# A gate folded into a product's weights by GpSimd, and a sum taken straight from PSUM

## The chip, the cores and the metric

The kernel runs on one core of one Trainium2 chip. The time is device time in microseconds (us) for one execution of the whole program. The five engines of the core (TensorE, VectorE, ScalarE, GpSimd, SyncE) each work through their own queue in order, and wait for one another by semaphores. In the profile PE is TensorE, PEld its weight loads, DVE VectorE, ACT ScalarE, POOL GpSimd, SP SyncE, which issues most transfers.

## The reference

One encoder block on 512 tokens of width 2048, in float32. Two token mixers (dilated window attention and chunked gated linear attention) read one normalised input; their gated outputs `a_out` and `g_out` are joined to 512 x 2048 and go through one output projection. What matters here is the end:

```python
y = jnp.concatenate([a_out, g_out], axis=-1) @ w_out[layer]
x = x + gate[:, None] * y
return rms_norm(x) * final_gain
```

`gate` is a vector of 2048, one factor per output column, the same for every token. So the factor of a column may be applied to that column of the product, or to that column of `w_out` ahead of the product.

## The kernel before

**Precision.** Each float32 operand is split into a high part, rounded to the format that TensorE takes at full rate, and a low part, the rest. ScalarE makes the high part (L493, in split_hi), VectorE the low one (L477, in split_lo). A product is then three matmuls: high times high, low times high, high times low (`three`, L231 to L233).

**The output projection.** The 2048 output columns are four column blocks j of 512, taken in two pairs, OUT_PAIRS = ((0, 1), (3, 2)). Each pair is computed by seven half-size products in place of eight (a Strassen scheme), in the order P1, P7, P6, P4, P5, P3, P2. Each product has four steps g; a step needs one block of weights of 128 x 1024 (two slices of 128 contracted rows by 512 columns). The blocks of the projection are numbered O0 to O55; O28 to O55 belong to the second pair, and O48 to O51 are P3's, O52 to O55 are P2's, the last product of all. P2's result goes to column block 3 only (`l` = 3), for row blocks 0 and 1 (128 tokens each). Row blocks 2 and 3 are finished during P3.

**How a block of weights arrives.** SyncE issues its load (L390) as soon as one of eight raw buffers is free; the last four blocks' loads wait for the low-half split of the block that used the buffer before. Then come the high half on ScalarE, into one of three buffers that TensorE must have left, and the low half on VectorE. The very first block of P2, O52, has buffers of its own, called `wlast`.

**The end.** While P3 runs, row blocks 2 and 3 get their last column block added (add_rest, L1611 to L1613) and are finished: `finish` makes the reciprocal root on ScalarE (L1585, L1586, into `rn`), scales on VectorE (L1595), ScalarE (L1596, L1598) and GpSimd (L1597), and stores. P2 then runs for row block 0 on 512 columns (accumulator `g3[0]`), and for row block 1 in two halves of 256 columns, each with an accumulator of its own, so that the first half can be added while TensorE works on the second. Row block 0 is added by add_rest and finished by finish_first. Row block 1 is added by add_half (L1644 multiplies the gate into the PSUM result, L1645 adds that to x), called once by first_half and once by finish_last, which also takes the sum of squares (L1658), makes the reciprocal root and scales and stores what is left. `gate_b` holds the gate on all 128 partitions; it is in place long before.

**Order.** TensorE's order is that of the program. On the other engines the compiler's scheduler chooses the order among the instructions that are ready, except in the parts under `tc.manual_schedule(engines=PLANNED)`, such as first_half and finish_last, which keep the order in which they are written. `last["hi"]` and `last["lo"]` chain the splits.

Of the kernel before, what the change touches and what calls it, by code (L numbers as in the profile page):

```python
# [13 lines left out]
AF = mybir.ActivationFunctionType  # L14
ALU = mybir.AluOpType
# [3 lines left out]
P = 128  # L19
# [112 lines left out]
OUT_PAIRS = ((0, 1), (3, 2))  # L132
# [60 lines left out]
def block_kernel(ctx: ExitStack, tc: tile.TileContext, a: dict):  # L193
    nc = tc.nc
# [20 lines left out]
    def PJ(name):  # L215
        return pp.tile([P, 512], F32, tag="pj", bufs=5, name=name)

    def PA(name):
        return pp.tile([P, 512], F32, tag="pa", bufs=3, name=name)

    mm = nc.tensor.matmul
    tt = nc.vector.tensor_tensor
    stt = nc.vector.scalar_tensor_tensor
    act = nc.scalar.activation
# [134 lines left out]
    groups = [(u, g) for u in ("qk2", "qk4", "qk6", "gk") for g in range(KT // 2)]  # L359
# [4 lines left out]
    raws, wts, low, last = {}, {}, set(), {}  # L364

    def fetch(i):
        if i < len(groups) and i not in raws:
            u, g = groups[i]
            if u == "O":
                raws[i] = out_fetch(g)  # L370
            elif u == "V":
                raws[i] = val_fetch(g)
            else:
                raws[i] = RAW(f"raw_{u}{g}", [2, 512])
                nc.sync.dma_start(raws[i], a["w_" + u][g])
# [86 lines left out]
    def whole(i):  # L462
        if i in second:
            t, e = raws[i], second.pop(i)
            tt(t, t, e, op=ALU.add)
# [14 lines left out]
    def split_hi(i):  # L480
        if i < len(groups) and i not in wts:
            fetch(i)
            u, g = groups[i]
            raw = raws[i].rearrange("p k c -> p (k c)")
            whole(i)
            dst = None
            if (u, g) == ("O", len(groups) - gi["O", 0] - 4):
                t = b8.tile([P, 2, 1024], F32R, tag="b8", name="wlast")
                dst = t[:, 0, :], t[:, 1, :]
            wts[i] = dst or (wp.tile([P, 1024], F32R, tag="whi", name=f"{u}{g}h"),  # L490
                             wp.tile([P, 1024], F32R, tag="wlo", name=f"{u}{g}l"))
            with tc.issue_after(last["hi"]) if u in ("V", "O") else nullcontext():
                last["hi"] = act(wts[i][0], raw, AF.Copy).ins  # L493
# [205 lines left out]
    for i in range(n):  # L699
        if i > 15:  # L700
            mm_task(i)
        st, k, j = chain[i]
# [14 lines left out]
    for i in range(n, 2 * n):  # L717
        mm_task(i)
        st, k, j = chain[i]
# [3 lines left out]
    for w in range(4):  # L723
        for kt in range(4):
            j, g = w // 2 * 4 + kt, w % 2
# [293 lines left out]
    def some_sums(name):  # L1019
        r = [sum_work.pop(0) for _ in range(SUMS_IN.get(name, len(sum_work)))]  # L1020
        n = len(r)
        loads = [(max(q - 1.1, 0.05) / n, x[0]) for q, x in enumerate(r)]
        return sorted(loads + [((q + 0.7) / n, x[1]) for q, x in enumerate(r)], key=lambda x: x[0])
# [278 lines left out]
    for n, p in (("qk2", 0), ("qk4", 2), ("qk6", 4)):  # L1302
        ps = unit(n, False, attention((p, p + 1)) + ([(0.05, shift_row)] if p == 2 else []))
# [9 lines left out]
    ps = unit("gk", False, attention((6, 7)) + [(0.88, lr_load)])  # L1313
# [138 lines left out]
    for j in range(2):  # L1452
        ps = unit(f"ag{j}", False, gla_head(1 + j) + some_sums(f"ag{j}"))
        gate_evict(ps, cat[j], f"a{j}", vbias[:, 4 * j:4 * j + 4])
    ps = unit("gg0", False, gla_head(3) + some_sums("gg0"))
# [44 lines left out]
    ps = unit("gg1", False, side + some_sums("gg1"))  # L1500
    gate_evict(ps, cat[3], "g1")
    mid.close()
    op = ctx.enter_context(tc.tile_pool(name="op", bufs=1, reuse_waits="tile"))
    for e in "hl":
        t = hp.tile([P, KT, 512], F32R, tag="h", name="c_" + e)
# [4 lines left out]
    gate_b = op.tile([P, 2048], F32, tag="gate", name="gate_b")  # L1510
# [11 lines left out]
    def E_(name):  # L1522
        return op.tile([P, 512], F32, tag="e", bufs=3, name=name)

    xo, x_pair, fgain = {}, {}, {}
    ssq = cst.tile([P, 4, 4], F32, tag="ssq", name="ssq")
# [23 lines left out]
    def keep(name, ps):  # L1550
        r = []
        for n, p_ in enumerate(ps):
            t = op.tile([P, 512], F32, tag="keep", bufs=7, name=f"{name}{n}")
            act(t, p_, AF.Copy)
            r.append(t)
        return r
# [12 lines left out]
    def summed(ps, kept, op_):  # L1569
        return lambda t: tt(t, ps, kept, op=op_)  # L1570

    def negated(ps, kept):
        return lambda t: stt(t, ps, -1.0, kept, op0=ALU.mult, op1=ALU.subtract)

    def first_squares(i, js):

        s = ssq[:, i, js[0]:js[0] + 1]
        for j in js[1:]:
            tt(s, s, ssq[:, i, j:j + 1], op=ALU.add)
        nc.vector.tensor_scalar(s, s, 1.0 / D, EPS, op0=ALU.mult, op1=ALU.add)  # L1580
        return s
# [26 lines left out]
    def add_rest(i, j, ps, op_):  # L1608

        x_, t = xo[i, j], E_(f"y{i}{j}")  # L1610
        tt(t, ps, gate_b[:, 512 * j:512 * j + 512], op=ALU.mult)  # L1611
        tt(x_, x_, t, op=op_)
        act(t, x_, AF.Square, accum_out=ssq[:, i, j:j + 1])  # L1613
# [21 lines left out]
    half_e = {}  # L1635

    def add_half(i, j, ps, z):

        c = slice(256 * z, 256 * z + 256)
        x_ = xo[i, j][:, c]  # L1640
        if not z:
            half_e[i] = E_(f"y{i}{j}")
        t = half_e[i][:, c]
        tt(t, ps, gate_b[:, 512 * j + 256 * z:512 * j + 256 * z + 256], op=ALU.mult)  # L1644
        tt(x_, x_, t, op=ALU.add)  # L1645
        return x_, t

    def first_half(i, j, ps, s):
        x_, t = add_half(i, j, ps, 0)
        act(t, x_, AF.Square, accum_out=ssq[:, i, j:j + 1])  # L1650
        tt(xo[i, 2], xo[i, 2], fgain[2], op=ALU.mult)
        stt(s, ssq[:, i, j:j + 1], 1.0 / D, s, op0=ALU.mult, op1=ALU.add)
# [77 lines left out]
    def more(pair, prod, g, fn, *args):  # L1730
        later(pair, prod, g, lambda: fn(*args))
# [6 lines left out]
    for pair, (l, r) in enumerate(OUT_PAIRS):  # L1738
        end = pair == 1
        g1 = [PA(f"g1{pair}{n}") for n in range(2)]  # L1740
        product(pair, "P1", g1, True, True)
        p1 = keep(f"p1{pair}", g1)
        gx = [PJ(f"gx{pair}{n}") for n in range(2)]
        product(pair, "P7", gx, True, True)
        p7 = keep(f"p7{pair}", gx)
        if end:
            for n in range(2):
                more(pair, "P6", n, x_with, n, l, p1[n], ALU.add)
                more(pair, "P6", 2 + n, x_with, 2 + n, r, p7[n], ALU.subtract)
        product(pair, "P6", g1, False, True)  # L1750
        u2 = keep(f"u2{pair}", g1)
        product(pair, "P4", gx, False, True)
        for n in range(2):
            more(pair, "P5", 1 + 2 * n, add_up, 2 + n, l, summed(gx[n], u2[n], ALU.add), True)
        product(pair, "P5", g1, False, True)
        v = keep(f"v{pair}", g1)
        for n in range(2):
            if not end:
                more(pair, "P3", 2 * n, add_up, 2 + n, r, negated(g1[n], p7[n]), True)
            else:  # L1760
                more(pair, "P3", 2 * n, add_rest, 2 + n, r, g1[n], ALU.subtract)
                more(pair, "P3", 2 * n + 1,
                     lambda n=n, l=l, r=r: finish(2 + n, r, first_squares(2 + n, [0, 1, l])))
        g2 = [PJ(f"g2{pair}{n}") for n in range(2)]
        product(pair, "P3", g2, True, True)
        if end:
            for i in range(gi["O", 0] + 2 * 4 * len(OUT_ORDER) - 3, len(groups)):
                split(i)
        for n in range(2):
            more(pair, "P2", n, add_up, n, r, summed(g2[n], v[n], ALU.subtract), not end)  # L1770
            if end:
                more(pair, "P2", n, sum_squares, n, [0, 1, r])
        g3 = [PJ(f"g3{pair}0"), PA(f"g3{pair}1")] + [PJ(f"g3{pair}2")] * end
        if not end:
            product(pair, "P2", g3, True, True)
            for n in range(2):
                more(pair + 1, "P1", 2 * n, add_up, n, l, summed(g3[n], p1[n], ALU.add), True)
            continue
        product(pair, "P2", g3, True, True, (0,))
        add_rest(0, l, g3[0], ALU.add)  # L1780
        finish_first(0, sq0[0])
        ah, al = ops["A12"]
        for z in range(2):
            c0, t = 256 * z, slice(P, 2 * P)
            for k in range(8):
                wh, wl = wts[gi["O", (pair * len(OUT_ORDER) + OUT_ORDER.index("P2")) * 4 + k // 2]]
                c = slice(512 * (k % 2) + c0, 512 * (k % 2) + c0 + 256)
                three(g3[1 + z][:, :256], ah[:, k, t], al[:, k, t], wh[:, c], wl[:, c], k == 0, k == 7)
        with tc.manual_schedule(engines=PLANNED):
            first_half(1, l, g3[1][:, :256], sq0[1])  # L1790
            finish_last(1, l, g3[2][:, :256], sq0[1])
# [71 lines left out]
```

## Time and profile before

| What | Value |
|---|---|
| median of 3 runs | 900.62 us (900.61 to 900.75) |
| the profiled execution | 900.47 us |
| its span in the profile | 898.7 us |
| TensorE busy | 889.1 us, 99% of the span |
| VectorE busy | 732.3 us, 81% |
| ScalarE busy | 500.9 us, 56% |
| GpSimd busy | 123.0 us, 14% |
| granted TensorE clock | 0.997 of full speed |

The span runs from the first to the last instruction that the profile shows; 1.8 us of the execution lie outside it. A share is the engine's busy time over the whole span, so it tells little of the last 40 us, where the edit lies. Busy time on TensorE is pipelined; a matmul's end is modelled. A wait is put down to the event that came last before it.

### The profile page before, as it was taken

The numbers are of one execution on the slowest core, as the hardware profiler recorded it, in microseconds if no ns is written. First come the engines' busy times: TensorE is split into PE (matmuls) and PEld (weight loads), VectorE is DVE, ScalarE is ACT, GpSimd is POOL, SyncE is SP. The second block draws the span as 40 slices with busy tenths as digits, with TensorE's granted clock in tenths as the row PEclk, the third lists the DMA queues.
The fourth block names the chain that finished last, engine by engine and source line by source line (L and its number), as shares of the span: only waits on it lengthen the run. The fifth ranks groups of instructions, "written<-read, shape, count | busy, mean of one in ns | idle before, by whom it ended". The sixth has DMA issues, their size and how long they took to land.

```text
span 898.7 us, 12367 instructions
## 1 busy us (share of the span) xinstructions
PE 889.1 (99%) x4190; PEld 741.5 (83%) x4190; DVE 732.3 (81%) x1221; ACT 500.9 (56%) x859; POOL 123.0 (14%) x219
## 2 busy tenths in 40 slices
PE   9999999999999999999999999999999999999996
PEld 7888788888888888888878888888888888888885
DVE  7998799878989989889668668595775749997797
ACT  5553533466755756756767554363644447655564
POOL 0000000024423333233100102111020100000001
PEclk9999999999999999999999999999999999999998
DMA  9998589398698899898878879678787898877853
GB/s 358 399 413 358 197 345 366 132 306 229 198 266 266 231 285 260 236 316 225 272 239 267 313 204 307 206 250 258 234 275 219 253 322 295 278 295 252 304 210 148
DMA packets 65547, 242.33 MB, mean 270 GB/s; under 512 B 9190, under 2 KB 11526, under 8 KB 55883
## 3 DMA queue, kind: packets, MB, share of 16 engines
q1 hardware_dynamic: 58724, 199.23, 61.5%
q0 software_dynamic: 6464, 42.01, 19.9%
q8 instruction: 33, 0.54, 0.2%
q10 hardware_dynamic: 296, 0.30, 0.1%
q14 instruction: 30, 0.25, 0.1%
HBM read 224.64 MB, written 51.47 MB: 307 GB/s over the span
## 4 chain that ended last, share of the span: by engine, by line
PE 98%; ACT 0%; DVE 0%; ACTq 0%; issue 0%
PE ps_qk L231 5%; PE ps_qk L233 5%; PE ps_qk L232 5%; PE g L231 4%; PE g L232 4%; PE g L233 4%; PE stb L233 3%; PE ps_gg L231 3%; PE ps_ag L231 3%; PE ps_ag L232 3%; PE ps_gg L232 3%; PE stb L232 3%; PE ps_ag L233 3%; PE ps_gg L233 3%; PE stb L231 3%; PE o L928 3%
## 5 line engine op out<-in xcount | busy, mean ns | idle before, releaser
L863 POOL TENSOR_SCALAR p<-p,st 128x32 f32<-128x32 f32 (+2 forms) x108 | 57.8, 544 | 160.2 <-DVE st L853 88.6
L327 DVE CUSTOM_DVE_ANT_0 cb<-cb,sb,c_bcond 128x2048 f32<-128x2048 f32 (+1 forms) x32 | 73.7, 2303 | 1.5 <-DMA cb<-in_wm 0.9
L850 ACT ACTIVATE p<-p,st 128x416 f32<-128x416 f32 x64 | 41.1, 642 | 56.0 <-DVE st L846 48.4
L428 POOL DMA_DIRECT2D T<-in_w_o x32 | 23.2, 724 | 155.4 <-ACT V2h L493 12.0
L886 ACT ACTIVATE pth<-t 128x384 fp32r<-128x384 f32 x64 | 30.9, 483 | 13.1 <-PE t L880 8.0
L887 DVE TENSOR_TENSOR ptl<-t,pth 128x384 fp32r<-128x384 f32 x64 | 35.2, 550 | 3.3 <-ACT pth L886 2.4
L880 PE MATMUL t<-c_ident,p 128*128 128x128 f32 x192 | 31.3, 272 | 0.0
L880 PEld LDWEIGHTS t<-c_ident,p 128*128 128x128 f32 x192 | 24.3, 139 | 7.8
L846 DVE CUSTOM_DVE_ANT_0 p<-s,g,st 128x256 f32<-128x256 f32 x64 | 27.7, 433 | 2.0
L846 DVE CUSTOM_DVE_ANT_0 p<-s,g 128x160 f32<-128x160 f32 x64 | 23.5, 368 | 4.6 <-PE s L839 4.2
L1597 POOL TENSOR_SCALAR x<-x,rn 128x512 f32<-128x512 f32 x2 | 2.9, 1444 | 146.0 <-ACT rn L1586 142.1
L428 POOL DMA_DIRECT2D T3V<-in_w_gv x8 | 5.5, 692 | 125.1 <-ACT qk21h L493 118.7
L838 PE MATMUL s<-ks,qh 128*128 128x416 f32 x64 | 22.5, 352 | 0.0
L327 DVE CUSTOM_DVE_ANT_0 rawg<-rawg,crow,gate 128x1024 f32<-128x1024 f32 x16 | 20.4, 1278 | 2.6 <-DMA rawg<-in_wg 2.5
L839 PE MATMUL s<-ks,ql 128*128 128x416 f32 x64 | 22.4, 350 | 0.0
L1104 ACT ACTIVATE sq<-st,sc 128x256 f32<-128x256 f32 x24 | 12.1, 505 | 17.3 <-DVE st L1099 8.9
L327 DVE CUSTOM_DVE_ANT_0 rawg<-rawg,crow,c_bcond 128x1024 f32<-128x1024 f32 x16 | 20.3, 1279 | 1.0 <-issue 1.0
L909 ACT ACTIVATE pth<-g 32x128 fp32r<-32x128 f32 x64 | 19.7, 308 | 1.6
L428 POOL DMA_DIRECT2D T<-T x16 | 9.1, 572 | 79.4 <-ACT V8h L493 13.0
L567 ACT ACTIVATE h_hi<-xt,shift 128x512 fp32r<-128x512 f32 x16 | 11.5, 722 | 10.3 <-DVE shift L327 9.5
L1372 DVE TENSOR_TENSOR vS<-rawS,vS 128x1024 fp32r<-128x1024 f32 x8 | 9.7, 1224 | 8.7 <-ACT vS L1371 8.5
L533 ACT ACTIVATE h_hi<-xt,scale 128x512 fp32r<-128x512 f32 (+1 forms) x18 | 12.5, 703 | 6.9 <-DVE scale L327 6.9
(1672 smaller groups left out, 3172.6 us busy)
## 6 DMA issues: line engine op xcount, KB each, us to landing
cb<-in_wm SPq DMA_DIRECT2D x31, 1024.0 KB, 11.4
T<-in_w_o POOLq DMA_DIRECT2D x32, 512.0 KB, 6.1
rawg<-in_wg SPq DMA_DIRECT2D x32, 512.0 KB, 5.3
raw_O<-in_w_o SPq DMA_DIRECT2D x32, 512.0 KB, 5.3
raw_qk<-in_w_qk SPq DMA_DIRECT2D x24, 512.0 KB, 4.9
raw_O<-T SPq DMA_DIRECT2D x24, 512.0 KB, 5.8
rawb<-in_w_sb SPq DMA_DIRECT2D x16, 512.0 KB, 7.9
rawv<-in_wv SPq DMA_DIRECT2D x16, 512.0 KB, 6.1
```

The lines of the kernel that those rows point to most:

```text
L231: mm(ps, lh, rh, start=first, stop=False, skip_group_check=more)
L232: mm(ps, ll, rh, start=False, stop=False, skip_group_check=more)
L233: mm(ps, lh, rl, start=False, stop=last, skip_group_check=more)
L327: return nc.vector.tensor_tensor_reduce(out=w, in0=w, in1=with_, op0=ALU.mult, op1=ALU.add, scale=1.0, scalar=init, accum_out=dst)
L428: move = nc.gpsimd.dma_start(dst, src, max_dma_last_dim=8192, **how).ins
L846: top = nc.vector.tensor_tensor_reduce(out=t[:, lo:hi], in0=ps[:, lo:hi], in1=gt[h][:, at:at + 2 * (hi - lo) - 1:2], op0=ALU.add, op1=ALU.min,
L850: act(t, t, AF.Exp, bias=st[:, 0:1], scale=-1.0, accum_out=st[:, 1:2])
L863: last["pool"] = nc.gpsimd.tensor_scalar(to, of, st[:, 2:3], 1.0, op0=ALU.mult, op1=ALU.mult).ins
L880: nc.tensor.transpose(pk[:, n_ * P:n_ * P + P], t[:, first_ + kt * P:first_ + kt * P + P], ident)
L886: act(hi, src, AF.Copy)
L887: tt(lo, src, hi.bitcast(F32), op=ALU.subtract)
L928: mm(po[:, P * a0:P * a1], vv[h // 4][:, c, h % 4, :], pt[:, at:at + (a1 - a0 - 1) * step + 1:step, :], start=n_ == z == 0, stop=False, sk ...
```

## The change

In split_hi, for the four blocks O52 to O55 (P2 of the second pair), GpSimd multiplies columns 256 to 511 of both slices of the raw block by the gate of column block 3, in place, ahead of the split into high and low halves. It is one instruction a block, on 128 x (2 x 256) elements; the gate operand is one row of 256 on each partition, read twice.

The second half of P2's result thus holds the gate already. add_half with z = 1 adds PSUM to x directly and leaves out the product with the gate. Row block 0 must take its two halves in different ways too, so the new add_parts stands in the place of add_rest: for z = 0 product and sum, for z = 1 the sum alone, then the Square with its sum as before.

```diff
@@ split_hi
             whole(i)
+            if u == "O" and i >= len(groups) - 4:
+                l = OUT_PAIRS[1][0]
+                g_ = gate_b[:, 512 * l + 256:512 * l + 512]
+                part_ = raws[i][:, :, 256:512]
+                nc.gpsimd.tensor_tensor(part_, part_, g_.unsqueeze(1).broadcast_to([P, 2, 256]), op=ALU.mult)
@@ add_half
         t = half_e[i][:, c]
-        tt(t, ps, gate_b[:, 512 * j + 256 * z:512 * j + 256 * z + 256], op=ALU.mult)
+        if z:
+            tt(x_, x_, ps, op=ALU.add)
+            return x_, t
+        tt(t, ps, gate_b[:, 512 * j:512 * j + 256], op=ALU.mult)
         tt(x_, x_, t, op=ALU.add)
         return x_, t
+
+    def add_parts(i, j, ps):
+
+        x_ = xo[i, j]
+        for z in range(2):
+            add_half(i, j, ps[:, 256 * z:256 * z + 256], z)
+        act(half_e[i], x_, AF.Square, accum_out=ssq[:, i, j:j + 1])
@@ the last pair, after P2 for row block 0
         product(pair, "P2", g3, True, True, (0,))
-        add_rest(0, l, g3[0], ALU.add)
+        add_parts(0, l, g3[0])
         finish_first(0, sq0[0])
```

## The prediction

> **What bounds the kernel now.** I read the page's busy shares first, then the chain of waits in its last 15 us, then the timelines of the engines around them.
>
> ```profile
> PE 889.1 (99%) x4190; PEld 741.5 (83%) x4190; DVE 732.3 (81%) x1221; ACT 500.9 (56%) x859; POOL 123.0 (14%) x219
> ```
>
> The whole is bound by TensorE. No matmul is added or removed, so only two things can move the time: a stall of TensorE, and what runs after its last matmul. The chain of waits shows that second stretch (start, us, what):
>
> ```profile
> 891.02 0.13 PE g L233
> 891.15 0.02 issue
> 891.17 0.44 DVE y L1644
> ...
> 891.63 0.44 DVE x L1645
> 892.09 0.48 DVE y L1658
> ```
>
> From 891.15, the end of the last matmul, everything is serial: gate product (L1644), sum into x (L1645), sum of squares (L1658), rsqrt, scaling, store. One link that goes shortens the end by its pitch, as long as nothing else arrives later. So the question is who else is nearly late. VectorE's timeline (start, us, engine, line, operation, tiles, shapes; in brackets the idle time before and its releaser):
>
> ```profile
> 867.30 1.23 DVE L477 TENSOR_TENSOR O49l<-raw_O,O49h 128x1024 fp32r<-128x1024 f32 x1 [0.63 <-ACT O49h L493]
> 869.16 0.69 DVE L1612 TENSOR_TENSOR x<-x,y 128x512 f32<-128x512 f32 x1
> 870.02 1.23 DVE L477 TENSOR_TENSOR O50l<-raw_O,O50h 128x1024 fp32r<-128x1024 f32 x1 [0.17 <-ACT O50h L493]
> 871.76 0.74 DVE L1595 SCALAR_TENSOR_TENSOR x<-x,rn,fgain 128x512 f32<-128x512 f32 x1
> 872.42 1.10 DVE L1612 TENSOR_TENSOR x<-x,y 128x512 f32<-128x512 f32 x1
> 873.99 1.23 DVE L477 TENSOR_TENSOR O51l<-raw_O,O51h 128x1024 fp32r<-128x1024 f32 x1 [0.47 <-ACT O51h L493]
> 875.56 1.23 DVE L477 TENSOR_TENSOR wlast<-raw_O,wlast 128x1024 fp32r<-128x1024 f32 x1 [0.34 <-ACT wlast L493]
> 876.70 1.22 DVE L477 TENSOR_TENSOR O53l<-raw_O,O53h 128x1024 fp32r<-128x1024 f32 x1
> 877.83 1.18 DVE L1595 SCALAR_TENSOR_TENSOR x<-x,rn,fgain 128x512 f32<-128x512 f32 x1
> ...
> 881.27 1.21 DVE L477 TENSOR_TENSOR O55l<-raw_O,O55h 128x1024 fp32r<-128x1024 f32 x1
> ...
> 885.67 0.68 DVE L1611 TENSOR_TENSOR y<-g,gate_b 128x512 f32<-128x512 f32 x1
> 886.39 0.69 DVE L1612 TENSOR_TENSOR x<-x,y 128x512 f32<-128x512 f32 x1
> ...
> 888.43 0.49 DVE L1628 TENSOR_SCALAR x<-xg,rn 128x512 f32<-128x512 f32 x1 [0.57 <-ACT rn L1586]
> ...
> 890.33 0.16 DVE L1652 SCALAR_TENSOR_TENSOR ssq<-ssq 128x1 f32<-128x1 f32 x1
> 891.17 0.42 DVE L1644 TENSOR_TENSOR y<-g,gate_b 128x256 f32<-128x256 f32 x1 [0.68 <-PE g L233]
> ```
>
> VectorE has almost no room. From 867 on its waits are 0.63, 0.17, 0.47 and 0.34, then none up to 0.57 ahead of L1628, and 0.68 ahead of the closing L1644. The 0.57 gives nothing back: L1628 waits for a chain (Square, two activations) that starts from VectorE's own L1612, so it moves with it. **Slack to the end: 0.68 us**, and no more.
>
> **The change, part by part.** *Removed at the end.* For row block 1, second half, the gate product goes and x takes PSUM directly: one instruction of 128x256 with one operand in PSUM, as L1644 has. It saves the pitch 891.17 to 891.63: **0.46 us**, all of it on the chain.
>
> *Row block 0* (add_parts for add_rest) has three 128x256 operations in place of two of 128x512. Before: 885.67 to the end of L1612 at 887.08, 1.41. After: by L1644's 0.42 each, with start distances of about 0.42 to 0.46, 1.3 to 1.4. I cost it at nothing. The Square behind it is unchanged.
>
> *Added: four products on GpSimd*, each 128x512 elements with two SBUF operands (weight half, gate), ahead of the split of blocks O52 to O55. When can they run? SyncE's timeline, its waits and the landing times of line 390:
>
> ```profile
> 856.15 1.80 SPq L390 DMA_DIRECT2D raw_O<-in_w_o  x2
> 860.68 0.33 SPq L390 DMA_DIRECT2D raw_O<-in_w_o  x1
> 863.06 0.33 SPq L390 DMA_DIRECT2D raw_O<-in_w_o  x1
> SPq L390 <- DVE O47l L477: 2.0, 1, 2.0
> DMA to landing us min/median/max: 3.4/4.4/5.2
> ```
>
> These four loads land between 856.15 + 3.4 = 859.6 and 863.06 + 5.2 = 868.3 (the last waits for O47l to free its buffer, so it slips with VectorE). GpSimd is empty there:
>
> ```profile
> 871.74 1.25 POOL L1597 TENSOR_SCALAR x<-x,rn 128x512 f32<-128x512 f32 x1 [142.11 <-ACT rn L1586]
> 876.84 1.64 POOL L1597 TENSOR_SCALAR x<-x,rn 128x512 f32<-128x512 f32 x1 [3.85 <-DVE wlast L477]
> ```
>
> So the products should run from about 861 to 870. The new wait is that of the high halves on ScalarE (L493): the first of them, wlast, starts only at 874.48, so 4 us of cover hide the wait (ScalarE's timeline):
>
> ```profile
> 873.87 0.61 ACT L1613 ACTIVATE y<-x 128x512 f32<-128x512 f32 x1
> ...
> 874.48 1.05 ACT L493 ACTIVATE wlast<-raw_O 128x1024 fp32r<-128x1024 f32 x1
> 875.43 0.27 ACT L1585 ACTIVATE rn<-ssq 128x1 f32<-128x1 f32 x1
> 875.61 1.04 ACT L493 ACTIVATE O53h<-raw_O 128x1024 fp32r<-128x1024 f32 x1
> 876.56 0.18 ACT L1586 ACTIVATE rn<-rn 128x1 f32<-128x1 f32 x1
> ...
> 879.75 1.06 ACT L493 ACTIVATE O55h<-raw_O 128x1024 fp32r<-128x1024 f32 x1 [0.69 <-PE g L232]
> ```
>
> Queued behind it on ScalarE stand the rsqrt of block 3 (L1585, L1586) and O53h; they would wait only if a product came after 874.5.
>
> *What a product does to VectorE.* VectorE's rows above show it at the GpSimd rows. L1612 takes 1.10 beside the first, 0.69 without; L1595 takes 1.18 beside the second, 0.74 without. The ends fit one reading: GpSimd's instruction waits for the running VectorE instruction (O53l ends at 877.92), runs about 0.56 to 878.48, and only then L1595 proceeds, to 879.01. A 128x512 GpSimd instruction of one operand thus delays VectorE by 0.41 to 0.44. [...]
>
> *Price of a two-operand product.* No row has one. Low end: that of one operand, 0.43. High end: the longest record above, 1.64, taken as if GpSimd held VectorE for all of it but the 0.13 by which the hold of 0.56 exceeds the delay of 0.43: 1.5. Between them I go by the grouped rows:
>
> ```profile
> L863 POOL TENSOR_SCALAR p<-p,st 128x416 f32<-128x416 f32 x16 | 9.8, 613 | 77.8 <-DVE st L853 43.6 <-PE s L839 17.1 <-issue 13.7
> L1097 POOL TENSOR_SCALAR dc<-st,sc 128x256 f32<-128x256 f32 x16 | 7.7, 479 | 29.1 <-DVE st L1094 24.1 <-DVE st L1099 4.9
> ```
>
> (613 - 479) / (416 - 256) = 0.84 ns per element, so a second operand of 512 elements adds 0.43: estimate **0.86 us a product**, nearest to the low end's rows. [...]
>
> *The sum.* VectorE in the stretch of the products is nearly always busy with two-operand SBUF work:
>
> ```profile
> 860.00:864.00 4.00, 4.00 (x19) 3.30 (x19) 4.00 (x6) 2.19 (x4) 0.00 (x0) 1.00 0.64 234
> 864.00:868.00 4.00, 4.00 (x20) 3.30 (x19) 3.22 (x8) 2.48 (x5) 0.00 (x0) 1.00 0.36 133
> 868.00:872.00 4.00, 4.00 (x19) 3.34 (x18) 3.80 (x6) 3.32 (x8) 0.26 (x1) 1.00 0.00 0
> ```
>
> (After the window's length stand TensorE, its weight loads, then VectorE: 4.00, 3.22, 3.80 of 4 us.) Four products: 4 x 0.86 = 3.44. Idle time takes up 0.63 (O49l) and 0.17 (O50l). Of 0.47 and 0.34 I count only 0.30 together: wlast's high half stands on ScalarE behind the Square of block 3 (L1613 at 873.87), which starts 0.35 after the end of L1612 at 873.52, about 0.05 of it latency, so ScalarE can yield only 0.30. VectorE's delay from 875.6 on: 3.44 - 0.63 - 0.17 - 0.30 = 2.34. It reaches the end unreduced, less the slack: 2.34 - 0.68 = 1.66 later, less 0.46 saved: **+1.20 us**.
>
> Does TensorE stall more? Its first uses of the low halves:
>
> ```profile
> 877.52 0.39 PE L233 MATMUL g<-O51l,c_h 128*128 128x512 f32 x1
> 884.32 0.39 PE L233 MATMUL g<-O55l,A12h 128*128 128x512 f32 x1
> ```
>
> O51l ends at 875.22, 2.30 ahead, and would slip 3.44 - 0.63 - 0.17 - 0.47 = 2.17: just in time. O55l ends at 882.48, 1.84 ahead, and slips 2.34: 0.5 of stall. TensorE would end 0.5 later, VectorE's queue is 1.66 beyond the old end; VectorE decides.
>
> The profiled execution took 900.47, the median is 900.62, 0.15 above. So 900.47 + 1.20 = 901.67, in terms of the median **901.8 us**. A measurement of this kernel can tell about 0.2%, 1.8 us, from no change; this is 0.13%.
>
> **The rivals.** *The products stay hidden.* If one delays VectorE by no more than (1.10 + 0.68) / 4 = 0.445, the delay ends within the slack and the 0.46 remains: 900.2. For it: the one-operand price of 0.43 is just below; a product beside L1611, which has one operand in PSUM, may cost little. Against: two operands, and 4.00 of 4 us busy.
>
> *GpSimd's order puts the products of O53 to O55 behind block 3's L1597*, which waits for rn; slower than before. From the point at which O53's product stands behind it this decides. L1597 ends at 878.48 and L1595 at 879.01; then products of 0.99 (0.56 + 0.43), with a VectorE instruction of 0.68 or 1.2 between: 880.0, about 881.7, about 883.9. O55h (1.06) and O55l (1.21) follow: 886.2 in place of 882.48, VectorE 3.7 late. 3.7 - 0.68 - 0.46 = +2.6: 903.2. For it: in the program L1597 of block 3 is written ahead of these splits. Against: the order is not the written one throughout (O53h at 875.61 stands between L1585 at 875.43 and L1586 at 876.56, though written after both), and the data are there 8 us before.
>
> *A dearer product* (1.0 to 1.5 each) with the order I expect: 4 x 1.0 - 1.10 - 0.68 - 0.46 = +1.8 up to 4 x 1.5 - 2.24 = +3.8, 902.4 to 904.4.
>
> **How the numbers follow.** Forecast (0.6 to 1.0 a product, 900.8 to 902.4) 0.50; hidden, 900.2 to 900.8, 0.25; dearer product 0.13; GpSimd's order 0.10; anything else, 0.02. The range 900.1 to 903.4 takes in the first two, the second rival and most of the dearer product, and leaves out some 0.07. Slower by over 0.2% (above 902.4): 0.13 + 0.10 + 0.01 = 0.24. Faster by over 0.2% needs 1.8 us where 0.46 is removed: 0.01. Same: 0.75.
>
> **What would show it.** Right: four GpSimd records of 128x512 between 861 and 871, VectorE instructions beside them 0.8 to 0.9 longer, the waits ahead of O49l and O50l gone, the closing L1645 started by VectorE's own L1652 instead of TensorE, 2 us after the last matmul or less. Wrong: the closing sum still starts 0.02 after TensorE's last matmul (hidden), products behind 878 with ScalarE waiting for GpSimd (the order), or TensorE gaps of over 0.5 ahead of O51l to O55l.

## The result, and the profile after

The changed kernel takes **901.94 us** (median of 22 runs), the kernel before 900.67 (22 runs beside them): ratio 1.0015, 95% interval 1.0009 to 1.0021. That is 1.27 us more, 0.14%; the interval, 0.8 to 1.9 us, lies above zero. The forecast was 901.8.

The profiled execution took 902.03, its span is 900.2. The columns are those of the prediction. From split_hi on the line numbers of the changed code are 5 higher than before, from add_half on 8 to 15 higher. First a part of the chain of waits near the end of the changed kernel:

```profile
892.59 0.60 DVE x L1666
893.19 0.13 DVE ssq L1667
893.33 0.34 DVE x L1650
893.67 0.02 issue
893.69 0.48 DVE y L1673
```

Before, the chain came from TensorE to the closing product; now it comes from VectorE's own queue (L1666, L1667), and the closing sum (L1650) is a single link. TensorE's timeline in the changed kernel shows where its last matmul ends:

```profile
892.39 0.28 PE L233 MATMUL g<-O55l,A12h 128*128 128x256 f32 x1
```

892.67, 0.57 ahead of the closing sum at 893.24. Then GpSimd's timeline of the changed kernel:

```profile
861.12 3.09 POOL L490 TENSOR_TENSOR raw_O<-raw_O,gate_b 128x512 f32<-128x512 f32 x2 [131.39 <-DMA raw_O<-in_w_o]
865.09 1.36 POOL L490 TENSOR_TENSOR raw_O<-raw_O,gate_b 128x512 f32<-128x512 f32 x1 [0.88 <-DMA raw_O<-in_w_o]
868.58 1.61 POOL L490 TENSOR_TENSOR raw_O<-raw_O,gate_b 128x512 f32<-128x512 f32 x1 [2.13 <-DVE ssq L1585]
```

The four products run from 861 to 870. The first and the third start when their block has landed; the second follows the first. The fourth is put down to VectorE's L1585, which had ended 0.7 us before, so what released it is not shown. VectorE's timeline of the changed kernel shows what lay beside them, and what became of it:

```profile
861.27 1.79 DVE L1568 TENSOR_TENSOR y<-y,gate_b 128x512 f32<-128x512 f32 x1
862.98 2.31 DVE L477 TENSOR_TENSOR O47l<-raw_O,O47h 128x1024 fp32r<-128x1024 f32 x1
865.21 1.78 DVE L1572 TENSOR_TENSOR x<-x,fgain 128x512 f32<-128x512 f32 x1
866.91 0.68 DVE L1569 TENSOR_TENSOR x<-y,x 128x512 f32<-128x512 f32 x1
...
868.95 1.78 DVE L1572 TENSOR_TENSOR x<-x,fgain 128x512 f32<-128x512 f32 x1
...
870.95 1.23 DVE L477 TENSOR_TENSOR O49l<-raw_O,O49h 128x1024 fp32r<-128x1024 f32 x1
...
875.15 0.99 DVE L1600 SCALAR_TENSOR_TENSOR x<-x,rn,fgain 128x512 f32<-128x512 f32 x1
876.07 0.68 DVE L1617 TENSOR_TENSOR x<-x,y 128x512 f32<-128x512 f32 x1
877.17 1.23 DVE L477 TENSOR_TENSOR O51l<-raw_O,O51h 128x1024 fp32r<-128x1024 f32 x1 [0.43 <-ACT O51h L498]
...
888.84 0.42 DVE L1652 TENSOR_TENSOR y<-g,gate_b 128x256 f32<-128x256 f32 x1
...
891.28 0.49 DVE L1633 TENSOR_SCALAR x<-xg,rn 128x512 f32<-128x512 f32 x1 [0.57 <-ACT rn L1591]
...
893.17 0.16 DVE L1667 SCALAR_TENSOR_TENSOR ssq<-ssq 128x1 f32<-128x1 f32 x1
893.24 0.41 DVE L1650 TENSOR_TENSOR x<-x,g 128x256 f32<-128x256 f32 x1
```

Four instructions are 1.1 us longer (1.79 and twice 1.78 against some 0.69, 2.31 against 1.23). The wait of 0.63 ahead of O49l is gone: it starts at 870.95 in place of 867.30. Row block 0 starts at 888.84 in place of 885.67, and the closing sum stands directly behind L1667.

### The profile page after: what moved, and what is told of

It is laid out like the page before. It is cut to its first block, busy times and chain, and to the rows that moved or that the text cites. A ratio compares the mean times of both kernels' runs of the same rounds, so it can differ in the third digit from the quotient of the medians.

```text
span 900.2 us, 12380 instructions
## 1 busy us (share of the span) xinstructions
PE 890.6 (99%) x4190; PEld 741.8 (82%) x4190; DVE 735.6 (82%) x1221; ACT 500.7 (56%) x859; POOL 127.3 (14%) x223
## 4 chain that ended last, share of the span: by engine, by line
PE 95%; DVE 2%; ACT 1%; issue 0%; ACTq 0%; DVEq 0%
PE ps_qk L231 5%; PE ps_qk L233 5%; PE ps_qk L232 5%; PE ps_gg L231 3%; PE stb L233 3%; PE ps_ag L231 3%; PE ps_ag L233 3%; PE stb L231 3%; PE ps_gg L232 3%; PE ps_ag L232 3%; PE ps_gg L233 3%; PE stb L232 3%; PE g L231 3%; PE g L232 3%; PE g L233 3%; PE o L933 3%
## 5 line engine op out<-in xcount | busy, mean ns | idle before, releaser
L490 POOL TENSOR_TENSOR raw_O<-raw_O,gate_b 128x512 f32<-128x512 f32 x4 | 6.1, 1520 | 134.4 <-DMA raw_O<-in_w_o 132.3
```

## The experiments

The theory on trial: the end gains one VectorE link of 0.46, and GpSimd's products hold VectorE up by more than its idle time and slack take in. The rivals: the new wait for GpSimd ahead of the splits costs the time; or the direct sum and the small operations do.

**direct_only: the end alone.** The changed kernel without its products; the gate is left out of the last 256 columns of P2's result.

```diff
-            if u == "O" and i >= len(groups) - 4:
...
-                nc.gpsimd.tensor_tensor(part_, part_, g_.unsqueeze(1).broadcast_to([P, 2, 256]), op=ALU.mult)
```

> The changed kernel without the four GpSimd products; the gate is thus left out of the last 256 columns of P2's result. Theory (the gain is one VectorE link at the end, the loss is GpSimd's products holding VectorE up): 0.46 under before, about 900.2 against 900.67; the closing sum starts 0.02 after TensorE's last matmul, and VectorE's waits ahead of O49l, O50l, O51l and wlast are back at about 0.63, 0.17, 0.47 and 0.34. Rival (the direct sum or the three small operations of row block 0 cost what was lost): it stays at 901 to 902.

900.16 (11 runs) against 900.52 (24 runs), ratio 0.9995, 0.9986 to 1.0004: 0.36 under, near the 0.46 expected, though the interval takes in no change. The profile says more. VectorE's timeline of this run:

```profile
867.26 1.22 DVE L477 TENSOR_TENSOR O49l<-raw_O,O49h 128x1024 fp32r<-128x1024 f32 x1 [0.63 <-ACT O49h L493]
...
885.64 0.41 DVE L1647 TENSOR_TENSOR y<-g,gate_b 128x256 f32<-128x256 f32 x1
885.98 0.41 DVE L1645 TENSOR_TENSOR x<-x,g 128x256 f32<-128x256 f32 x1
886.30 0.42 DVE L1648 TENSOR_TENSOR x<-x,y 128x256 f32<-128x256 f32 x1
...
891.14 0.42 DVE L1645 TENSOR_TENSOR x<-x,g 128x256 f32<-128x256 f32 x1 [1.00 <-PE g L233]
891.60 0.48 DVE L1668 CUSTOM_DVE_ANT_0 y<-x,ssq 128x256 f32<-128x256 f32 x1
```

The closing sum waits for TensorE again, and the sum of squares follows 0.46 after its start, not 0.92. The three small operations start 0.34 and 0.32 apart and end at 886.72, where the two large ones ended at 887.08; hence the wait for TensorE is 1.00, not 0.68. Neither the direct sum nor row block 0 costs anything, so the second rival falls.

**lock_only: the products alone.** The kernel before, with the four products written to a tile that nothing reads.

```diff
+            if u == "O" and i >= len(groups) - 4:
...
+                beside = op.tile([P, 2, 256], F32, tag="beside", bufs=1, name="beside")
+                nc.gpsimd.tensor_tensor(beside, part_, g_.unsqueeze(1).broadcast_to([P, 2, 256]), op=ALU.mult)
```

> The kernel before, with the same four two-operand GpSimd products beside it, written to a tile that nothing reads, so no engine waits for them and the result is the reference's. Theory (GpSimd holds VectorE up): the VectorE instruction beside each product is 1.09 longer as in the changed kernel, VectorE is about 3.1 late at row block 0 (here without the 0.32 that the three small operations saved), less 0.77 of slack: 2.3 above before, about 903.0. Rival (the loss comes from the new wait for GpSimd ahead of the splits): no loss, 900.7.

903.0 (8 runs) against 900.52 (24 runs), ratio 1.0026, 1.0016 to 1.0036: 2.5 above the kernel before, with no engine waiting for a product. VectorE's timeline of this run:

```profile
861.37 1.79 DVE L1569 TENSOR_TENSOR y<-y,gate_b 128x512 f32<-128x512 f32 x1
863.08 2.31 DVE L477 TENSOR_TENSOR O47l<-raw_O,O47h 128x1024 fp32r<-128x1024 f32 x1
...
893.62 0.16 DVE L1658 SCALAR_TENSOR_TENSOR ssq<-ssq 128x1 f32<-128x1 f32 x1
893.69 0.42 DVE L1650 TENSOR_TENSOR y<-g,gate_b 128x256 f32<-128x256 f32 x1
...
894.61 0.48 DVE L1664 CUSTOM_DVE_ANT_0 y<-x,ssq 128x256 f32<-128x256 f32 x1
```

The lengths are those of the changed kernel, and again the closing instruction stands behind VectorE's own L1658. So the products cost this much without any wait for them.

**one_operand and write_only: the same waits, another GpSimd instruction.** The changed kernel with another instruction in the place of the product: in one_operand the first of the two added lines, in write_only the second.

```diff
-                nc.gpsimd.tensor_tensor(part_, part_, g_.unsqueeze(1).broadcast_to([P, 2, 256]), op=ALU.mult)
+                nc.gpsimd.tensor_scalar(part_, part_, 1.0, 1.0, op0=ALU.mult, op1=ALU.mult)
+                nc.gpsimd.memset(part_, 0.0)
```

> The changed kernel with a one-operand GpSimd instruction on the same data at the same place (times 1.0), so every wait of the change is there; the gate is left out of the last 256 columns of P2's result. Theory (the price is the time for which GpSimd holds VectorE up): 0.43 a product as beside L1597, 1.7 in all, swallowed by idle time (about 1.1) and the slack of 0.77: 900.2. Rival (the wait for GpSimd ahead of the splits, whatever GpSimd does): 901.9 as in the changed kernel.

> The changed kernel with a GpSimd memset to zero in place of each product: the same waits, but nothing is read; the second half of P2's result is thus zero. If only a GpSimd instruction that reads SBUF holds VectorE up: VectorE's instructions beside the memsets keep 0.69 and 1.23, time 900.2. If any GpSimd instruction does: they are 0.3 to 0.5 longer, and the time is 900.2 all the same, within the slack. If the wait alone costs: 901.9.

899.92 and 900.09 (11 runs each) against 900.56 (21 runs), both ratios 0.9994, 0.9985 to 1.0003. With every wait in place the cost of the products is gone, so the wait as such is not the cause. VectorE's timeline of one_operand, then of write_only, at the same instructions:

```profile
862.80 1.10 DVE L1572 TENSOR_TENSOR x<-x,fgain 128x512 f32<-128x512 f32 x1
863.82 1.09 DVE L1569 TENSOR_TENSOR x<-y,x 128x512 f32<-128x512 f32 x1
```

```profile
861.79 1.22 DVE L477 TENSOR_TENSOR O47l<-raw_O,O47h 128x1024 fp32r<-128x1024 f32 x1
862.93 0.68 DVE L1572 TENSOR_TENSOR x<-x,fgain 128x512 f32<-128x512 f32 x1
```

With one operand they take 1.10 and 1.09 against 0.68 and 0.69, 0.41 longer each. (The other two products of that run began beside 128x1 instructions; O48l and O49l behind them are only 0.19 and 0.28 longer, 1.42 and 1.51 against 1.23.) The four memsets lie between 860.8 and 867.4, and no VectorE instruction is longer. So in these runs it is a GpSimd instruction that reads SBUF that holds VectorE up, and the product of two operands, 1.09, costs more than twice what the instruction of one operand costs.

**two_of_four: half the dose.** The changed kernel with the products of O53 and O55 alone.

```diff
-            if u == "O" and i >= len(groups) - 4:
+            if u == "O" and i >= len(groups) - 4 and i % 2:
```

> The changed kernel with products on O53 and O55 alone; the gate is left out of the second half of O52 and O54. Theory (delays add up on VectorE, idle time and slack at the end swallow the first part): 2 x 1.09 = 2.2, less about 1.1 to 1.3 of idle time and 0.32 of row block 0, is below the slack of 0.77, so nothing of it arrives: 900.2, as with no product at all. Rival (each product costs the end the same share): half way between 900.2 and 901.94, about 901.1.

900.02 (11 runs) against 900.52 (24 runs), ratio 0.9994, 0.9985 to 1.0003. Half the products cost the end nothing that can be measured. VectorE's timeline of this run, all of it some 0.7 later than in direct_only from O46l on (860.12 against 859.40):

```profile
863.64 1.79 DVE L1572 TENSOR_TENSOR x<-x,fgain 128x512 f32<-128x512 f32 x1
...
868.28 2.10 DVE L477 TENSOR_TENSOR O49l<-raw_O,O49h 128x1024 fp32r<-128x1024 f32 x1
...
891.86 0.42 DVE L1650 TENSOR_TENSOR x<-x,g 128x256 f32<-128x256 f32 x1 [0.32 <-PE g L233]
```

The two products make VectorE's instructions 1.10 and 0.87 longer, and of the 1.00 of slack in direct_only 0.32 is left. The end pays no fixed share per product; it pays what passes idle time and slack.

**early: the products elsewhere, three times.** GpSimd multiplies the second halves in a tile of their own during earlier products, stores them to DRAM, and the late loads of O52 to O55 take columns 256 to 511 from there.

```diff
+        if (pair, what) == (1, "21"):
+            src = block(pair, what, g)
+            nc.sync.dma_start(t[:, :, :256], src[:, :, :256])
+            d = gated[g]
+            nc.sync.dma_start(t[:, :, 256:512], bass.AP(d.tensor, d.offset, [[512, P], [256, 2], [1, 256]]))
...
+    def gate_weights(g):
...
+        nc.gpsimd.tensor_tensor(t, t, g_.unsqueeze(1).broadcast_to([P, 2, 256]), op=ALU.mult)
...
+        nc.sync.dma_start(d, t.rearrange("p k c -> p (k c)"))
```

> Same result as the changed kernel, the products elsewhere: during P5 of the first pair GpSimd multiplies the second halves of the four blocks in a tile of their own and they are stored to DRAM; the late loads of O52 to O55 take columns 256 to 511 from there. 2 MB more are read and 1 MB more written. Theory (what counts is that VectorE is full where the products lie and has no more than 0.8 of slack to the end): VectorE loses about 1.1 a product there, which TensorE does not feel, and the end has the 0.46: 900.2. Rival (the products or the additional transfers delay the splits of P5 or P3): TensorE gaps near P5, 901 or more.

908.92 (4 runs) against 900.52 (24 runs), ratio 1.0087, 1.0073 to 1.0101: a miss, and for a reason of the experiment's own. (It reads 1 MB more, four loads of 256 KB, not the 2 MB expected.) GpSimd's timeline, SyncE's waits and TensorE's waits of this run:

```profile
770.60 10.56 POOL L1748 TENSOR_TENSOR gated<-gated,gate_b 128x512 f32<-128x512 f32 x1 [41.16 <-DMA gated<-in_w_o]
```

```profile
SPq L1751 <- POOL gated L1748: 27.1, 4, 11.0
```

```profile
PE g L233 <- DVE O17l L484: 5.0, 1, 5.0
PE g L233 <- DVE O26l L484: 1.2, 1, 1.2
```

Each store stood in SyncE's queue waiting for GpSimd, up to 11.0 us, and the loads of the weights behind it waited too; TensorE waited 5.0 and 1.2 and ended 8.8 later than before (its last matmul starts at 899.66 against 890.86). So load and store went to GpSimd's own queue:

> Same result as the changed kernel. The four products run from the end of the first pair's P2 to P7 of the second pair, in one tile of their own; load, product and store of each stand on GpSimd's own queue, so nothing of them stands in SyncE's queue (where, in the run before, each store waited for GpSimd and held the loads of the weights behind it). The late loads of O52 to O55 take columns 256 to 511 from the stored result. Theory: VectorE has 1 to 3 us of idle time in every 10 there and the splits are 3 us ahead of TensorE, so nothing stalls, and the end has its 0.46: 900.2, closing sum 0.02 after the last matmul. Rival (the early place costs by itself): TensorE gaps between 800 and 850, 901 or more.

900.76 (11 runs) against 900.69 (15 runs), ratio 1.0000, 0.9991 to 1.0009. The expected gain of 0.46 is not there. The scheduler had drawn the products even further ahead, to 754 to 803, and in the profiled execution, a long one of 902.70, TensorE still waited 0.8 for O26l. So each load was held back to the second pair's P1 or P7:

> As the run before (same result as the changed kernel, products through GpSimd's queue into DRAM), but each load waits for a high half of the second pair's P1 or P7 on ScalarE, so that the products lie at 810 to 850, where VectorE is busy 7 to 9 us in 10, and not at 755 to 803 where it is full. Theory: no TensorE gap from them, VectorE caught up before 860, the closing sum 0.02 after the last matmul with about 1.0 of wait before it: 900.2, 0.4 to 0.5 under the kernel before. Rival (the place does not matter, an additional load and store do): 900.7 or more.

900.54 (11 runs) against 900.59 (21 runs), ratio 1.0002, 0.9993 to 1.0011; the changed kernel in the same series took 902.07 (after_again, 11 runs), ratio 1.0018, 1.0009 to 1.0027:

> The changed kernel itself beside the run above on one chip. Theory: 901.9, 1.7 above the version with early products.

In the profile of after_again the products met other VectorE instructions, and these are together longer by as much as in the first profile: 2.28 against 1.23, 1.78 and 1.77 against 0.69, and an instruction of 128x1 that takes 0.15 elsewhere:

```profile
868.12 1.28 DVE L1584 TENSOR_TENSOR ssq<-ssq 128x1 f32<-128x1 f32 x1
```

So the delay hardly depends on the VectorE instruction of two SBUF operands that is held up: 1.13 at 128x1, 1.08 at 128x1024 (2.31 against 1.23). VectorE's timeline of early_paced:

```profile
891.52 0.42 DVE L1652 TENSOR_TENSOR x<-x,g 128x256 f32<-128x256 f32 x1 [1.01 <-PE g L233]
891.98 0.48 DVE L1675 CUSTOM_DVE_ANT_0 y<-x,ssq 128x256 f32<-128x256 f32 x1
```

The end is as the theory says, 1.01 of wait and one link, but TensorE arrives 0.35 later than before (891.52 against 891.17). It lost 0.6 at O42l: its first matmul of O41l starts 0.30 earlier than before (850.02 against 850.32), its second of O42l 0.31 later (854.03 against 853.72). The profile of early, too, has a wait of TensorE at O42l (0.3 in both), although its last product ran at 815, so what causes it is not shown. With the same result early_paced is 1.5 faster than the changed kernel, so where the products stand accounts for the loss. Against the kernel before, the 0.4 to 0.5 expected cannot be measured: 900.54 lies between the theory's 900.2 and the rival's 900.7. No version with the right result is measurably faster than the kernel before.

## Why the prediction was right, point by point

*What bounds the end.* Right: VectorE's queue, with less than 1 us of slack, decides; lock_only shows the loss by itself. In its profile the sum of squares starts 2.3 later than before (894.61 against 892.09, less 0.20 by which that run was late at O46l). It lacks the link saved, 0.47, and the 0.32 gained at row block 0; less these, 2.3 becomes 1.5, what the changed kernel's profile shows.

*The place of the products and the new wait.* Right: 861 to 870, ahead of every L1602, and ScalarE never waits for one. The rival of GpSimd's order did not occur.

*The mechanism.* Right: a GpSimd instruction that reads holds VectorE up (0.41 in one_operand, and in the rows of before L1612 at 1.10 against 0.69); one that only writes does not (write_only, 0.68 stays 0.68). A VectorE instruction with an operand in PSUM was not held up where the kernel before has one beside such a GpSimd instruction: L846 of 128x256 at 390.37 takes 0.41 within the time of L863 (390.16 to 391.02), and 0.42 at 401.60, where GpSimd runs nothing.

*The price of a product.* Mis-sized: 0.86 by the slope of one-operand rows, measured 1.79 - 0.69, 2.31 - 1.23 and twice 1.78 - 0.69: 4.36 for four, 1.09 each. The rows of one operand could not show it: from one operand to two the delay grows by 0.68 (0.41 to 1.09), where the slope gave 0.43. The price thus lies where the prediction had put its rival of a dearer product (1.0 to 1.5); that rival's time of 902.4 or more did not come, because more of the delay was taken up than either sum allowed for.

*The rest of the sum.* The changed run was 0.10 late already at O46l (the first of these lines is of the kernel before, the second of the changed one), so shifts are taken less 0.10:

```profile
859.43 1.22 DVE L477 TENSOR_TENSOR O46l<-raw_O,O46h 128x1024 fp32r<-128x1024 f32 x1
859.53 1.22 DVE L477 TENSOR_TENSOR O46l<-raw_O,O46h 128x1024 fp32r<-128x1024 f32 x1
```

| Term | Predicted, us | Measured, us | From |
|---|---|---|---|
| four products | 3.44 | 4.36 | lengths above |
| taken up by idle time | 1.10 | 1.29 | 4.36 less 888.84 - 885.67 - 0.10 |
| row block 0, gained | 0 | 0.32 | 885.67 to 888.43 before, 888.84 to 891.28 after |
| slack to the end | 0.68 | 0.77 | start of L1652 (L1667 after) to closing start: 0.84 before, 0.07 after |
| link saved | 0.46 | 0.47 | closing start to L1658 or L1673: 0.92 before, 0.45 after |
| sum | +1.20 | +1.51 | the sum of squares: 893.69 - 892.09 - 0.10 = 1.50 |

So 0.92 too little for the products stood against 0.61 too little for what softens them. The medians differ by 1.27, and the interval of 0.8 to 1.9 takes in both sums. That the forecast came within 0.1 us of the measured change is luck: two errors, each a large part of the change, nearly cancelled. (The prediction held 1.8 us to be the least that can be told from no change; 22 runs on each side told 1.27.) "I cost it at nothing" for row block 0 was the second wrong step. Its three instructions of 256 elements, none of which needs the result of the one just ahead of it, start 0.34 and 0.33 apart; of the two of 512 before, the second needs the first, and starts 0.72 behind it.

The idle time, too, was not taken up where the prediction had it. The waits ahead of O51l and wlast, counted at 0.30, gave 0.05 (0.47 and 0.34 became 0.43 and 0.33), because ScalarE's high halves slipped with VectorE (O51h starts at 876.10 in place of 872.91). Some 0.9 went ahead of O49l and O50l, where 0.80 was counted. Of the rest, 0.17 comes from GpSimd's first scaling instruction (L1597, now L1602): it holds L1600 up by 0.25 (0.99 against 0.74), where before it held L1612 up by 0.42 (1.10 against 0.68).

*TensorE.* Stalls were predicted at 0.5 in all. It ends at 892.67 against 891.14 before (the last record there starts at 890.86 and takes 0.28): 1.53 later, or 1.4 without the common 0.10. VectorE's delay was 3.1, where the prediction had 2.17 at O51l and 2.34 at O55l, and passes the 2.30 and 1.84 that these had in hand. The longest waits of its weight loads in the changed kernel:

```profile
PEld g L233 <- DVE O51l L477: 0.9, 1, 0.9
PEld g L233 <- DVE O55l L477: 0.5, 1, 0.5
PEld g L233 <- DVE O49l L477: 0.3, 1, 0.3
```

A TensorE gap of over 0.5 ahead of O51l was named as a sign of being wrong, and it came: O51l's first matmul starts at 878.46, 0.86 after the one ahead of it, where 0.23 is usual. VectorE is 0.57 later still, so this did not show in the time; TensorE is the next bound, close behind.

## What to carry to other kernels

In these runs work on an idle GpSimd was not free where it read SBUF while VectorE ran instructions of two SBUF operands: a product of 128x512 with two operands cost VectorE 1.09 us, an instruction with one operand 0.41, a memset nothing. Price such work as VectorE time. That price can be read from the length of VectorE instructions beside GpSimd records already in a trace, but only for an instruction of the same kind; the rows of one operand gave 0.86 for the product that took 1.09. What such a delay costs is what exceeds idle time and slack up to the end, so half of the work can cost nothing measurable (two_of_four) and the whole more than it gains. Whoever moves the work should look at the queue of its transfers: in early a store that waited on SyncE for up to 11.0 us held up the loads behind it.

## What the runs showed of the hardware that was not expected

In two runs a product that was ready had to wait while several VectorE instructions started ahead of it: eight in early, where its record takes 10.56 us from 770.60, and six in early_pool:

```profile
776.47 9.02 POOL L1751 TENSOR_TENSOR gated<-gated,gate_b 128x512 f32<-128x512 f32 x1 [3.96 <-DMA gated<-in_w_o]
```

VectorE's instructions of 128x1024 went on every 1.14 us, none longer, until one with an operand in PSUM came (784.25 in early_pool) or VectorE had nothing to do (780.01 in early). The other products of these two runs are 1.30 to 1.76 long; those of 767.02 and 801.05 in early_pool came in behind the VectorE instruction that was running, and the instruction after that one takes 2.31 against 1.22 and 1.78 against 0.69. A run made for it put nine such products into the same stretch of the kernel before, reading O8 to O16:

```diff
+            if u == "O" and 8 <= g < 17:
...
+                nc.gpsimd.tensor_tensor(beside, raws[i][:, :, 256:512], g_, op=ALU.mult)
```

> The kernel before with nine GpSimd products (two operands, 128x512) that read the raw blocks O8 to O16 as they land and write a tile that nothing reads, in the stretch in which VectorE has one 128x1024 instruction of two SBUF operands after another (755 to 782 in the kernel before). If GpSimd gets its turn at the end of the running VectorE instruction, as at 861 to 870: no product longer than 1.2 + 1.1 = 2.3, each VectorE instruction behind it 1.1 longer, VectorE up to 9 late and TensorE stalled behind it. If it can be passed over as long as VectorE's next such instruction stands ready: products of 5 us and more, few VectorE instructions longer, little time lost.

It took 906.59 (a single run, against 900.69 in 15 runs). GpSimd's and VectorE's timelines of it:

```profile
754.21 16.92 POOL L489 TENSOR_TENSOR beside<-raw_O,gate_b 128x512 f32<-128x512 f32 x8 [24.45 <-DMA gate_b<-garow]
```

```profile
756.52 2.31 DVE L477 TENSOR_TENSOR O8l<-raw_O,O8h 128x1024 fp32r<-128x1024 f32 x1
758.76 2.31 DVE L477 TENSOR_TENSOR O9l<-raw_O,O9h 128x1024 fp32r<-128x1024 f32 x1
```

Here GpSimd and VectorE took turns, product by product, and each of eight VectorE instructions in a row took 2.30 to 2.32. That is the first alternative, not the second. What makes GpSimd be passed over in the other two runs stays open; the size of VectorE's instructions and the stretch by themselves do not do it.
